# Modulation products of one decoder layer: the attention gate and the FFN shift and scale made on VectorE in 1024-column pieces, and four FFN block pairs split over two halves of their rows

## The chip, the cores and the metric

One core of a Trainium2 chip runs the whole layer as one program. The metric is the device time of one execution in microseconds; lower is better. Three executions of the kernel before took 1274.52, 1274.74 and 1276.62 us, median 1274.74 us.

## What is computed

One layer for 256 tokens of width 2048, all in float32. A conditioning vector `c` makes six modulation rows of 2048 numbers; they shift, scale and gate the attention part (`_a`) and the feed-forward part (`_f`).

```python
mod = jax.nn.silu(c) @ w_ada[l] + b_ada[l]          # w_ada: 2048 x 12288
shift_a, scale_a, gate_a, shift_f, scale_f, gate_f = jnp.split(mod, 6, axis=-1)
h = rms_norm(x, g_attn_pre) * (1 + scale_a) + shift_a
proj = h @ w_in                                      # 2048 x 5456
...                                                  # two kinds of attention, 8 heads each
x = x + gate_a * rms_norm(mixed @ w_o, g_attn_post)
h = rms_norm(x, g_ffn_pre) * (1 + scale_f) + shift_f
ff = (silu(h @ w_gate) * (h @ w_up)) @ w_down        # 2048 x 5632, and back
x = x + gate_f * rms_norm(ff, g_ffn_post)
```

## The kernel before, in words

**Weights.** Every weight matrix is read once from HBM, a megabyte at a time (`wload`, L148), into one of five `raw` buffers. ScalarE copies a K pair to `whi` in a reduced format (L168), VectorE makes the rest `wlo` by a subtraction (L169), and each product becomes three TensorE passes (`mm3`, L176 to L182). Three pairs of `whi`/`wlo` buffers exist, so VectorE can be at most three such tiles ahead of TensorE. One 512-column, four-K-tile load is 24 passes of 512 columns.

**Modulation.** `ada_block` (L191) queues the product of silu(c) with a block of `w_ada` columns as units of one megabyte, each a load and a use. With `on_pe` the use is done on TensorE: the K tiles go to four column groups of the array (L225), the four partial rows end in one PSUM bank, ScalarE brings them out (L242), and for a gate the bias row comes by one more product (L240). Without `on_pe` VectorE does it: one multiply-and-add per K tile over all 128 partitions into `aacc` (L231, L233). Either way a finishing product on TensorE sums over partitions: `ada_cols` (L275) makes columns of shift and gain*(1+scale) (L282 after TensorE, L286 after VectorE), `ada_gate` (L296) makes the gate row (L301). The attention's own shift and scale are always made on TensorE. Of the attention gate (`Ga`) blocks 0 and 1 are made on TensorE and 2 and 3 on VectorE; of the FFN shift and scale (`modF`) blocks 0, 1 and 3 on TensorE and 2 on VectorE; the FFN gate (`Gf`) wholly on VectorE. Blocks are 512 columns: a unit has four K tiles, and on VectorE four instructions.

**Order.** `ada_step` takes units off that queue: during the last `w_in` group one or two per weight block (`RATE`, L737), one per block in the output projection (`side`, L789), `FRATE` per block in the split FFN blocks (L884). While the last `w_in` group and the first two column blocks of `w_o` run, attention proceeds by stages (`attn_step`, L430): rotary embedding (`rope`, L351), indexer scores and top-k, softmax, products with V. Each engine runs its instructions in the order in which they stand; a scheduler with a timeline of its own sets that order when the program is built.

**From attention to FFN.** `tail_pair` (L770) ends `w_o` with token tile 0 first. `residual` (L836) then makes x1: the block times its gate (L768), the square sums, `ry`, x1 (L843), the diagonal matrix `dg` (L848). `h2_tiles` (L826) needs `dg`, and the FFN's first products need its result. `NSPLIT` gate/up column blocks are first multiplied with K tiles 0 to 7 alone (L875), put aside in `part` by ScalarE (L887), and completed later by a VectorE addition (L909); so the second half of `modF` may come late.

Of the kernel before, what the change touches and what calls it, by code (L numbers as in the profile page):

```python
# [22 lines left out]
P = 128  # L23
S = 256
T = 2
# [14 lines left out]
GA_DVE = (2, 3)  # L40
F_DVE = (2,)
# [3 lines left out]
FRATE = 2  # L45
# [4 lines left out]
NSPLIT = 2  # L50
# [6 lines left out]
def layer(ctx, tc, x, c, positions, w_ada, b_ada, g_attn_pre, g_attn_post, g_ffn_pre,  # L57
# [26 lines left out]
    # ---- constants  # L84
# [20 lines left out]
    # ---- vectors, brought to columns  # L105
# [33 lines left out]
    c33 = ct([P, KT, 33], "c33")  # L139
    POOL.memset(c33, 0.0)  # L140
    DVE.tensor_copy(c33[:, :, 1], csil)
# [5 lines left out]
    # ---- weights: fp32 tiles split exactly into two fp32r parts  # L147
    def wload(rows, k0, nk, c0, n, more=None):  # L148
        """Rows k0.. of a block of columns: {(K tile, 512-column block): (hi, lo)}."""
# [4 lines left out]
        for a in range(0, nk, 2):  # L154
            m = min(2, nk - a)
            step = min(n, 1024 // m)
            for b in range(0, n, step):
                w = min(step, n - b)
                if more is not None and a + m == nk:
                    hi = more.tile([P, 1024], F32R, tag="xhi", name=nm("xhi"))  # L160
                    lo = more.tile([P, 1024], F32R, tag="xlo", name=nm("xlo"))
# [22 lines left out]
    # ---- adaLN modulation  # L184
# [6 lines left out]
    def ada_block(col0s, n, on_pe, finish, brow=None):  # L191
        """Queues the products of silu(c) with n columns of w_ada at each of col0s, a megabyte at a
        time. On the tensor engine the K tiles go to four column groups, and the products of the
        i-th block end as the rows 32*j+i of one bank."""
# [5 lines left out]
        def new_acc(b):  # L200
            st["acc", b] = wp.tile([P, 512], F32, tag="aacc", name=nm("aacc"), bufs=2)

        def load(b, u):
            if u == 0 and brow is not None and (b == 0 or not on_pe):
                new_acc(b)
                if not on_pe:
                    POOL.memset(st["acc", b], 0.0)
                SP.dma_start(st["acc", b][0:1], brow)
# [65 lines left out]
    # shift and scale as columns: shift, and gain*(1+scale)  # L274
# [20 lines left out]
    # gate times the post gain, the same row on every partition  # L295
    def ada_gate(G, chunk, col, on_pe):  # L296
        c0 = chunk * D + col

        def finish(accs):
            ps = tr_bank()  # L300
            PE.matmul(ps, lhsT=ones, rhs=accs[0], start=True, stop=True)  # L301
            DVE.tensor_tensor(G[:, col:col + 512], ps, G[:, col:col + 512], op=ALU.mult)

        ada_block([c0], 512, on_pe, finish, b_ada[0:1, c0:c0 + 512])

    # ---- first norm, transposed
# [15 lines left out]
    def make_h(H, src, mod, k, qs=slice(0, S), lk=None, on_act=True):  # L322
        """A K tile of gain*(1+scale)*x + shift, split in two; the work shared by ACT and DVE."""
# [13 lines left out]
    ph1 = ExitStack()  # L337
# [646 lines left out]
```

## Time and profile before

| | |
|---|---|
| runs | 1274.52, 1274.74, 1276.62 us |
| profiled execution, first to last instruction (its span) | 1272.5 us |
| what lies around the span, taken from the median of the runs | 2.2 us |
| TensorE busy | 1233.9 us, 97% of the span |
| VectorE busy | 774.3 us, 61% |
| ScalarE busy | 560.9 us, 44% |
| DMA queue q1 | 309.14 MB, 70.7% of 16 engines |
| mean granted TensorE clock | 0.993 of full speed |

The execution that was profiled has no time of its own beside its span; the median of the runs is 2.2 us above that span. The busy time of TensorE is modelled at the ends of its matmuls, so a full row of nines says that it was always fed and not how fast it went; the starts of two neighbours in the order of time say that. An average such as VectorE's 61% covers stages with different limits, so the stages are read one by one below.

### The profile page before, as it was taken

To read this page: it belongs to the slowest core of one execution; us is meant where nothing else is said; L and a number is where in the kernel's file an instruction comes from. 1 tells how busy PE (TensorE), PEld (TensorE's weight loads), DVE (VectorE), ACT (ScalarE), POOL (GpSimd) and SP (SyncE) were. 2 spreads that over 40 slices of the span, in tenths; PEclk is the share of its full clock that TensorE was granted. 3 is DMA by queue.
4 is the path that set the end of the run, shared out by engine and by line. 5 is a ranking of instruction groups with operands and counts; after the bars stand their busy time and mean duration, and the time that the engine had idled before them with its cause. 6 is when DMAs were issued, how large, how long until landed. Compare 5 with 4: busy or idle time off the path is not lost.

```text
span 1272.5 us, 15272 instructions
## 1 busy us (share of the span) xinstructions
PE 1233.9 (97%) x5938; PEld 950.3 (75%) x5938; DVE 774.3 (61%) x1160; ACT 560.9 (44%) x806; POOL 21.4 (2%) x55
## 2 busy tenths in 40 slices
PE   4999999999999999899999999999999999999996
PEld 3666666777666786688887888888888888888885
DVE  3576455898598683758867545754455454445565
ACT  4733333345345543764444444444444334444442
POOL 1000000000000000200000000000000000000000
PEclk8999999999999999999999999999999999999998
DMA  9999997978687487858878656766556555565541
GB/s 307 339 343 327 347 381 278 314 263 321 211 285 268 142 329 289 306 167 286 282 264 290 200 193 222 251 227 198 176 189 199 190 188 190 194 198 182 184 164 66
DMA packets 160090, 310.13 MB, mean 244 GB/s; under 512 B 5785, under 2 KB 19978, under 8 KB 158738
## 3 DMA queue, kind: packets, MB, share of 16 engines
q1 hardware_dynamic: 159938, 309.14, 70.7%
q8 instruction: 46, 0.75, 0.2%
q14 instruction: 26, 0.21, 0.0%
q10 hardware_dynamic: 80, 0.02, 0.0%
HBM read 307.05 MB, written 2.10 MB: 243 GB/s over the span
## 4 chain that ended last, share of the span: by engine, by line
PE 88%; DMA 4%; DVE 4%; issue 1%; ACT 1%; SPq 1%; POOL 0%; DVEq 0%; POOLq 0%; ACTq 0%
PE mm L181 26%; PE mm L178 26%; PE mm L182 25%; PE ad L225 5%; DMA raw<-in_w_ada_dram 4%; DVE aacc L233 2%; DVE wlo L169 1%; PE tr L474 1%; PE tr L411 1%; PE tr L918 1%; PE tr L830 1%; SPq L211 1%; PE tr L392 1%; PE tr L301 0%; PE tr L282 0%
## 5 line engine op out<-in xcount | busy, mean ns | idle before, releaser
L169 DVE TENSOR_TENSOR wlo<-raw,whi 128x1024 fp32r<-128x1024 f32 (+1 forms) x383 | 462.3, 1212 | 338.6 <-ACT whi L168 337.7
L168 ACT ACTIVATE whi<-raw 128x1024 fp32r<-128x1024 f32 (+1 forms) x383 | 400.3, 1050 | 522.4 <-PE mm L182 458.1
L181 PE MATMUL mm<-wlo,h 128*128 128x512 f32 (+1 forms) x1056 | 416.8, 395 | 1.9 <-DVE wlo L169 1.9
L182 PE MATMUL mm<-whi,h 128*128 128x512 f32 (+1 forms) x1056 | 409.9, 389 | 0.2 <-DVE h L335 0.2
L178 PE MATMUL mm<-whi,h 128*128 128x512 f32 (+1 forms) x1056 | 381.4, 394 | 2.4 <-ACT h L330 1.4
L181 PEld LDWEIGHTS mm<-wlo,h 128*128 128x128 f32 x1056 | 198.9, 188 | 62.5 <-issue 9.5
L178 PEld LDWEIGHTS mm<-whi,h 128*128 128x128 f32 x1056 | 196.8, 188 | 63.2 <-issue 13.6
L182 PEld LDWEIGHTS mm<-whi,h 128*128 128x128 f32 x1056 | 198.3, 188 | 42.5 <-issue 3.0
L181 PE MATMUL mm<-wlo,gT 128*128 128x512 f32 x348 | 135.8, 390 | 0.0
L182 PE MATMUL mm<-whi,gT 128*128 128x512 f32 x348 | 135.4, 389 | 0.0
L178 PE MATMUL mm<-whi,gT 128*128 128x512 f32 x348 | 123.0, 390 | 0.0
L233 DVE SCALAR_TENSOR_TENSOR aacc<-raw,csil,aacc 128x512 f32<-128x512 f32 x126 | 94.1, 746 | 23.8 <-DMA raw<-in_w_ada_dram 22.5
L225 PE MATMUL ad<-raw,c 128*32 128x512 f32 (+2 forms) x640 | 79.6, 537 | 9.9 <-DMA raw<-in_w_ada_dram 9.9
L733 DVE TENSOR_TENSOR PR<-mm,PR 128x512 f32<-128x512 f32 (+1 forms) x88 | 57.1, 669 | 41.2 <-PE mm L182 41.0
L182 PEld LDWEIGHTS mm<-whi,gT 128*128 128x128 f32 x348 | 65.3, 188 | 13.8 <-issue 0.2
L181 PEld LDWEIGHTS mm<-wlo,gT 128*128 128x128 f32 x348 | 65.3, 188 | 13.7 <-issue 0.2
L178 PEld LDWEIGHTS mm<-whi,gT 128*128 128x128 f32 x348 | 65.3, 188 | 13.4
L181 PE MATMUL mm<-wlo,mixT 128*128 128x512 f32 x124 | 49.1, 397 | 0.0
L178 PE MATMUL mm<-whi,mixT 128*128 128x512 f32 x124 | 47.5, 400 | 0.6 <-ACT mixT L587 0.6
L182 PE MATMUL mm<-whi,mixT 128*128 128x512 f32 x124 | 46.4, 399 | 0.0
L225 PEld LDWEIGHTS ad<-raw,c 128*32 128x32 f32 x640 | 17.6, 116 | 36.4 <-issue 31.3
L181 PEld LDWEIGHTS mm<-wlo,mixT 128*128 128x128 f32 x124 | 23.3, 188 | 7.8 <-issue 2.5
(195 smaller groups left out, 678.8 us busy)
## 6 DMA issues: line engine op xcount, KB each, us to landing
raw<-in_w_ada_dram SPq DMA_DIRECT2D x96, 1024.0 KB, 7.1
raw<-in_w_gate_dram SPq DMA_DIRECT2D x44, 1024.0 KB, 5.2
raw<-in_w_up_dram SPq DMA_DIRECT2D x44, 1024.0 KB, 5.1
raw<-in_w_down_dram SPq DMA_DIRECT2D x44, 1024.0 KB, 5.2
raw<-in_w_in_dram SPq DMA_DIRECT2D x39, 1024.0 KB, 6.9
raw<-in_w_o_dram SPq DMA_DIRECT2D x16, 1024.0 KB, 5.0
xx<-in_x_dram SPq DMA_DIRECT2D x2, 1024.0 KB
x<-in_x_dram SPq DMA_DIRECT2D x2, 1024.0 KB, 4.7
```

The costliest lines, as they stand in the source:

```text
L168: ACT.activation(hv, src, AF.Copy)
L169: DVE.tensor_tensor(lv, src, hv.bitcast(F32), op=ALU.subtract)
L178: i = PE.matmul(ps, lhsT=hi, rhs=whi, start=start, stop=False)
L181: PE.matmul(ps, lhsT=hi, rhs=wlo, start=False, stop=False)
L182: PE.matmul(ps, lhsT=lo, rhs=whi, start=False, stop=stop)
L211: SP.dma_start(st[b, u], ada_w[u * kk * P:(u + 1) * kk * P, col0s[b]:col0s[b] + n] .rearrange("(k p) n -> p k n", p=P))
L225: PE.matmul(st["ps"][32 * j:32 * j + 32, :n], lhsT=c33[:, k, 1 - b:33 - b], rhs=w, start=(b == 0 and k < 4), stop=(b == nb - 1 and k >= 12 ...
L233: DVE.scalar_tensor_tensor(acc, w, csil[:, k:k + 1], acc, op0=ALU.mult, op1=ALU.add)
L392: PE.transpose(tr[:, i * P:(i + 1) * P], PR[:, t, c0:c0 + P], ident)
L411: PE.matmul(sc[i][:, SEG[t]], lhsT=st["q"][r, (2 * j + t) * P:(2 * j + t + 1) * P], rhs=ikT[r, :P * (t + 1)], start=True, stop=True)
L474: PE.matmul(sc[i][:, SEG[t]], lhsT=l, rhs=r, start=False, stop=(t == T - 1))
L733: DVE.tensor_tensor(dst, banks[c0][t][:, :n], dst, op=ALU.add)
```

## The change

Three things change, and some buffers are moved to make room.

1. `ada_gate` no longer takes a TensorE path, and `ada_cols` is called for the FFN with `on_pe` false. Blocks are 1024 columns, so a unit is two K tiles and two VectorE instructions. `aacc` holds 1024 columns. The FFN gate, on VectorE before too, is made in 1024-column pieces as well.
2. `NSPLIT` goes from 2 to 4, and `FRATE` from 2 to 1: all four gate/up column blocks of the first FFN group are split over two halves of their rows (K tiles 0 to 7, then 8 to 15).
3. Buffers: the two last tiles of a `tail_pair` share one tile with the second `part` buffer; the silu(c) columns `c33` take the place of `nsel` until top-k begins; the rotary temporaries take the two `on` buffers of the differential heads instead of one pair of their own.

```diff
-GA_DVE = (2, 3)
-F_DVE = (2,)
-FRATE = 2
+FRATE = 1
-NSPLIT = 2
+NSPLIT = 4
...
-                    hi = more.tile([P, 1024], F32R, tag="xhi", name=nm("xhi"))
-                    lo = more.tile([P, 1024], F32R, tag="xlo", name=nm("xlo"))
+                    both = more.tile([P, 2, 1024], F32R, tag="part", name=nm("xhl"))
+                    hi, lo = both[:, 0], both[:, 1]
...
-            st["acc", b] = wp.tile([P, 512], F32, tag="aacc", name=nm("aacc"), bufs=2)
+            st["acc", b] = wp.tile([P, 1024], F32, tag="aacc", name=nm("aacc"), bufs=2)
...
-    def ada_gate(G, chunk, col, on_pe):
+    def ada_gate(G, chunk, col, n):
         c0 = chunk * D + col
         def finish(accs):
-            ps = tr_bank()
-            PE.matmul(ps, lhsT=ones, rhs=accs[0], start=True, stop=True)
-            DVE.tensor_tensor(G[:, col:col + 512], ps, G[:, col:col + 512], op=ALU.mult)
-        ada_block([c0], 512, on_pe, finish, b_ada[0:1, c0:c0 + 512])
+            for a in range(0, n, 512):
+                ps = tr_bank()
+                PE.matmul(ps, lhsT=ones, rhs=accs[0][:, a:a + 512], start=True, stop=True)
+                g = G[:, col + a:col + a + 512]
+                DVE.tensor_tensor(g, ps, g, op=ALU.mult)
+        ada_block([c0], n, False, finish, b_ada[0:1, c0:c0 + n])
...
-        m1 = pp.tile([P, P], F32, tag="rp1", name=nm("rp1"), bufs=1)
-        m2 = pp.tile([P, P], F32, tag="rp2", name=nm("rp2"), bufs=1)
+        m = pp.tile([P, 2, P], F32, tag="on", name=nm("rp"), bufs=2)
+        m1, m2 = m[:, 0], m[:, 1]
...
-    for b in range(4):
-        ada_gate(Ga, 2, b * 512, b not in GA_DVE)
+    for b in range(2):
+        ada_gate(Ga, 2, b * 1024, 1024)
     need_ga = len(units)
-    for b in range(4):
-        ada_cols(modF, 3, bF, gF, b * 512, 512, b not in F_DVE)
-        if b == 1:
+    for b in range(2):
+        ada_cols(modF, 3, bF, gF, b * 1024, 1024, False)
+        if b == 0:
             need_f1 = len(units)
...
-            for b in range(4):
-                ada_gate(Gf, 5, b * 512, False)
+            for b in range(2):
+                ada_gate(Gf, 5, b * 1024, 1024)
```

The program that is built moves instructions. On VectorE, where attention's indexer scores (`score`) end and top-k is about to begin, this stood before (`wlo` are weight splits, `PR` the sums of the input projection):

```order
L447 COPY skT<-tr_2658 128x256
L422 SCALAR_TENSOR_TENSOR score<-rl_2654,iwS,score 128x128
L422 SCALAR_TENSOR_TENSOR score<-rl_2654,iwS,score 128x256
L448 TENSOR_TENSOR score<-score,mask 128x384
L422 SCALAR_TENSOR_TENSOR score<-rl_2711,iwS,score 128x128
L422 SCALAR_TENSOR_TENSOR score<-rl_2711,iwS,score 128x256
L169 TENSOR_TENSOR wlo_3141<-raw_3138,whi_3140 128x1024
L733 TENSOR_TENSOR PR<-mm_2940,PR 128x512
L169 TENSOR_TENSOR wlo_3145<-raw_3138,whi_3144 128x1024
```

And this stands there now, in the changed kernel's line numbers (`aacc` is a modulation product):

```order
L448 COPY skT<-tr_2600 128x256
L228 SCALAR_TENSOR_TENSOR aacc_2992<-raw_2990,csil,aacc_2992 128x1024
L422 SCALAR_TENSOR_TENSOR score<-rl_2592,iwS,score 128x128
L422 SCALAR_TENSOR_TENSOR score<-rl_2592,iwS,score 128x256
L228 SCALAR_TENSOR_TENSOR aacc_2992<-raw_2990,csil,aacc_2992 128x1024
L422 SCALAR_TENSOR_TENSOR score<-rl_2596,iwS,score 128x128
L422 SCALAR_TENSOR_TENSOR score<-rl_2596,iwS,score 128x256
L228 SCALAR_TENSOR_TENSOR aacc_2992<-raw_2995,csil,aacc_2992 128x1024
L485 TENSOR_REDUCE mx_2841<-tr_2832 128x1 x2
L449 TENSOR_TENSOR score<-score,mask 128x384
L164 TENSOR_TENSOR wlo_3268<-raw_3265,whi_3267 128x1024
```

The sixteen products of one whole modulation column block stand here, each between two steps of attention or two weight splits; before, no modulation product stood between the first score of this phase and the end of top-k.

On TensorE, where `w_o` ends and the FFN begins, this stood before (the last passes of `w_o`, modulation units, then the products with `dg`):

```order
L181 MATMUL mm_3923<-xlo_4194,mixT 128x512
L182 MATMUL mm_3923<-xhi_4193,mixT 128x512
L225 MATMUL ad_4170<-raw_4412,c_112 32x512 x4
L225 MATMUL ad_4170<-raw_4418,c_112 32x512 x4
L225 MATMUL ad_4170<-raw_4458,c_112 32x512 x4
L830 MATMUL tr_4283<-dg_3918,x_3897 128x128 x4
```

And now:

```order
L176 MATMUL mm_3824<-xhl_4070,mixT 128x512
L177 MATMUL mm_3824<-xhl_4070,mixT 128x512
L831 MATMUL tr_4159<-dg_3819,x_3798 128x128 x4
L831 MATMUL tr_4180<-dg_3819,x_3798 128x128 x4
L173 MATMUL mm_4249<-whi_4253,h_3814 128x512
```

The three modulation units are gone from between the last pass and the first product that waits for `dg`. On VectorE, in the `residual` of token tile 0 that makes this `dg` (`sst`, `rs` and `x` are its steps), this stood before:

```order
L768 TENSOR_TENSOR y<-mm_3922,Ga 128x512
L839 TENSOR_REDUCE sst<-ssy 128x1
L144 TENSOR_SCALAR rs_4228<-sst 128x1
L843 SCALAR_TENSOR_TENSOR x_3897<-y,ry,x_3897 128x1024 x2
L169 TENSOR_TENSOR wlo_4377<-raw_4374,whi_4376 128x1024
```

And now:

```order
L769 TENSOR_TENSOR y<-mm_3823,Ga 128x512
L840 TENSOR_REDUCE sst<-ssy 128x1
L228 SCALAR_TENSOR_TENSOR aacc_4049<-raw_4287,csil,aacc_4049 128x1024
L139 TENSOR_SCALAR rs_4104<-sst 128x1
L164 TENSOR_TENSOR wlo_4254<-raw_4251,whi_4253 128x1024
L228 SCALAR_TENSOR_TENSOR aacc_4049<-raw_4287,csil,aacc_4049 128x1024
L769 TENSOR_TENSOR y<-mm_3822,Ga 128x512
L844 SCALAR_TENSOR_TENSOR x_3798<-y,ry,x_3798 128x1024 x2
```

Two modulation products, a weight split and a block of token tile 1 now stand between the square sums and x1.

## Rows read from the trace of the kernel before

**Rows 1.** The page's head: busy time of the engines, and the span in 40 slices of 31.8 us, in tenths.
```profile
span 1272.5 us, 15272 instructions
PE 1233.9 (97%) x5938; PEld 950.3 (75%) x5938; DVE 774.3 (61%) x1160; ACT 560.9 (44%) x806; POOL 21.4 (2%) x55
PE   4999999999999999899999999999999999999996
DVE  3576455898598683758867545754455454445565
```

**Rows 2.** Busy time of each engine in four stretches: the last `w_in` group with attention and the first two columns of `w_o`; the rest of `w_o`, the residual and the first FFN products; the FFN's start; the rest of the span. Columns: stretch and length, busy us (instructions) of PE, PEld, DVE, ACT and POOL, granted clock, DMA share, GB/s.
```profile
198.00:450.00 252.00, 246.97 (x1278) 171.99 (x1270) 187.96 (x461) 113.28 (x248) 8.61 (x10) 1.00 0.74 258
450.00:533.00 83.00, 79.30 (x389) 57.41 (x388) 53.37 (x82) 40.17 (x71) 6.65 (x11) 1.00 0.86 317
533.00:577.00 44.00, 44.00 (x214) 36.95 (x214) 25.74 (x43) 28.38 (x48) 0.53 (x1) 1.00 0.58 193
577.00:1273.00 696.00, 684.77 (x3055) 565.51 (x3053) 397.24 (x401) 293.32 (x313) 2.17 (x4) 0.99 0.61 206
```

**Rows 3.** The modulation products on TensorE (L225) in two of these stretches: busy us (records) of PE and PEld. A unit of 512 columns is eight records.
```profile
198.00:450.00 252.00, 26.53 (x176) 4.21 (x168) 1.00 0.74 258
450.00:533.00 83.00, 11.23 (x64) 1.85 (x64) 1.00 0.86 317
```

**Rows 4.** One such unit among the passes of `w_in` on TensorE, in order of time: start us, us, what, count.
```profile
287.26 0.61 PE L178 MATMUL mm<-whi,h 128*128 128x512 f32 x2
287.80 1.06 PE L225 MATMUL ad<-raw,c 128*32 128x512 f32 x8
288.80 0.50 PE L181 MATMUL mm<-wlo,h 128*128 128x512 f32 x1
289.13 0.39 PE L182 MATMUL mm<-whi,h 128*128 128x512 f32 x1
```

**Rows 5.** Groups by line and shape: count, busy us, mean ns of one, idle before.
```profile
L240 PE MATMUL ad<-aacc,ident 1*32 1x512 f32 x4 | 2.1, 600 | 0.0
L286 PE MATMUL tr<-ones,aacc 128*128 128x1 f32 x16 | 2.1, 218 | 0.0
L843 DVE SCALAR_TENSOR_TENSOR x<-y,ry,x 128x1024 f32<-128x1024 f32 x4 | 5.0, 1281 | 1.8 <-POOL ry L145 1.8
L231 DVE TENSOR_SCALAR aacc<-raw,csil 128x512 f32<-128x512 f32 x2 | 1.0, 478 | 0.0
L313 DVE TENSOR_SCALAR xx<-xx,rx 128x2048 f32<-128x2048 f32 x2 | 2.5, 1283 | 0.8 <-POOL rx L145 0.8
L909 DVE TENSOR_TENSOR part<-mm,part 128x512 f32<-128x512 f32 x8 | 5.2, 681 | 0.0
```

**Rows 6.** The modulation products on VectorE (L233) as a whole, and their busy us (instructions) in four stretches.
```profile
L233 DVE SCALAR_TENSOR_TENSOR aacc<-raw,csil,aacc 128x512 f32<-128x512 f32 x126 | 94.1, 746 | 23.8 <-DMA raw<-in_w_ada_dram 22.5
198.00:450.00 252.00, 35.04 (x47) 1.00 0.74 258
450.00:533.00 83.00, 11.19 (x15) 1.00 0.86 317
577.00:1273.00 696.00, 47.83 (x64) 0.99 0.61 206
376.00:450.00 74.00, 11.21 (x15) 1.00 0.63 219
```

**Rows 7.** What VectorE waited for between 198 and 450 us (waited for: us in total, times, longest), the first rows.
```profile
DVE wlo L169 <- ACT whi L168: 36.7, 28, 4.5
DVE score L422 <- ACT rl L415: 6.0, 4, 3.3
DVE mx L484 <- PE tr L474: 4.6, 6, 2.0
```

**Rows 8.** Four short stretches and one longer, columns as in rows 2: VectorE's highest shares, its share in the middle of attention's end, and that end as a whole.
```profile
250.00:300.00 50.00, 50.00 (x254) 36.50 (x252) 46.41 (x117) 23.68 (x57) 3.54 (x4) 1.00 0.85 296
400.00:430.00 30.00, 25.00 (x137) 18.93 (x135) 23.10 (x60) 16.14 (x48) 2.11 (x2) 1.00 0.56 193
450.00:475.00 25.00, 25.00 (x118) 20.90 (x118) 23.55 (x31) 11.39 (x17) 0.00 (x0) 1.00 0.94 352
575.00:625.00 50.00, 50.00 (x228) 41.48 (x227) 46.36 (x57) 24.05 (x26) 0.00 (x0) 1.00 0.83 290
376.00:450.00 74.00, 68.97 (x385) 52.41 (x383) 53.28 (x137) 40.80 (x111) 3.86 (x4) 1.00 0.63 219
```

**Rows 9.** From the last pass of `w_o` to the first product with `dg`: TensorE, then VectorE's steps of the residual, in order of time; in brackets the idle time before and what ended it.
```profile
511.32 0.39 PE L182 MATMUL mm<-xhi,mixT 128*128 128x512 f32 x1
511.64 2.78 PE L225 MATMUL ad<-raw,c 128*32 128x512 f32 x24
516.57 0.38 PE L830 MATMUL tr<-dg,x 128*128 128x128 f32 x1 [2.15 <-POOL dg L848]
507.64 0.15 DVE L839 TENSOR_REDUCE sst<-ssy 128x1 f32<-128x4 f32 x1
507.82 0.15 DVE L144 TENSOR_SCALAR rs<-sst 128x1 f32<-128x1 f32 x1
508.64 2.48 DVE L843 SCALAR_TENSOR_TENSOR x<-y,ry,x 128x1024 f32<-128x1024 f32 x2 [0.66 <-POOL ry L145]
```

More of the change, by code (lines that the diff above doesn't have):

```diff
@@ L138, in layer @@
     ACT.activation(csil, cols[:, 0:16], AF.Silu)
-    c33 = ct([P, KT, 33], "c33")
-    POOL.memset(c33, 0.0)
-    DVE.tensor_copy(c33[:, :, 1], csil)
     def rstd(o, ss, n, width, eng=DVE):
@@ L206, in load @@
                 if not on_pe:
-                    POOL.memset(st["acc", b], 0.0)
-                SP.dma_start(st["acc", b][0:1], brow)
+                    POOL.memset(st["acc", b][:, :n], 0.0)
+                SP.dma_start(st["acc", b][0:1, :n], brow)
             raw = wp.tile([P, 2048], F32, tag="raw", name=nm("raw"), bufs=RAW)
@@ L293, in ada_cols @@
         ada_block([chunk * D + col, (chunk + 1) * D + col], n, on_pe, finish)
-    def ada_gate(G, chunk, col, on_pe):
+    def ada_gate(G, chunk, col, n):
         c0 = chunk * D + col
         def finish(accs):
-            ps = tr_bank()
-            PE.matmul(ps, lhsT=ones, rhs=accs[0], start=True, stop=True)
-            DVE.tensor_tensor(G[:, col:col + 512], ps, G[:, col:col + 512], op=ALU.mult)
-        ada_block([c0], 512, on_pe, finish, b_ada[0:1, c0:c0 + 512])
+            for a in range(0, n, 512):
[4 more added lines that the diff above has]
+        ada_block([c0], n, False, finish, b_ada[0:1, c0:c0 + n])
+    ph1 = ExitStack()
+    pp = ph1.enter_context(tc.tile_pool(name="pp", bufs=1))
+    c33 = pp.tile([P, 528], F32, tag="nsel", name="c33").rearrange("p (k n) -> p k n", n=33)
+    POOL.memset(c33, 0.0)
+    DVE.tensor_copy(c33[:, :, 1], csil)
     ssx = ct([P, T], "ssx")
@@ L335, in make_h @@
         DVE.tensor_tensor(lo, hf[:, :n], hi.bitcast(F32), op=ALU.subtract)
-    ph1 = ExitStack()
-    pp = ph1.enter_context(tc.tile_pool(name="pp", bufs=1))
     PR = pp.tile([P, T, NPROJ], F32, tag="PR", name="PR")
@@ L369, in layer @@
     score = pp.tile([P, 384], F32, tag="score", name="score")
-    nsel = pp.tile([P, 384], F32, tag="nsel", name="nsel")
     nselb = pp.tile([P, 384], BF16, tag="nselb", name="nselb")
@@ L441, in top_k @@
         m8 = pp.tile([P, T, 8], F32, tag="m8", name="m8")
+        nsel = pp.tile([P, 528], F32, tag="nsel", name="nsel")[:, :384]
         def head():
```

## The prediction

> **What bounds the kernel now.** I read the page's head first. TensorE is busy 1233.9 us of a span of 1272.5 us, and from the second to the last but one of the 40 slices it shows a nine or an eight; VectorE is at 61% [rows 1]. So over the span TensorE is the bound and a microsecond taken off it is worth a microsecond, as long as VectorE stays beneath it. But the change puts work on VectorE in one part of the span only, so I read busy time by stages [rows 2]. The reader is to see there that VectorE does 188.0 us in the 252 us from 198 to 450 us (75%) and 53.4 us in the 83 us that follow (64%), and that TensorE loses 5 us and 3.7 us in these two. After 577 us VectorE is at 57% under a TensorE that hardly stops. I call the two stretches A and B; everything that the change moves lies in them or costs nothing.
>
> **What leaves TensorE.** In A stand 176 records of modulation products, in B 64, eight to a unit: 22 units and 8 units [rows 3]. The change takes 32 units off (two blocks of the attention gate with four units, three FFN blocks with eight), so two lie ahead of 198 us. The price of one: from the start of a unit to the start of the next pass is 1.00 us, and from 287.26 to 289.13 us three passes and a unit took 1.87 us, where a pass among passes starts 0.23 us after the other; the unit with its borders costs 1.19 us [rows 4]. Between 1.0 and 1.2 I take 1.1: units that stand together have fewer borders. That is 24.2 us in A, 8.8 in B, 2.2 before. The two bias products go too, 2.1 us, in A [rows 5]. Added are twelve finishing products, since VectorE leaves a separate sum for shift and for scale (32 in place of 20): eight programmed products of this kind took 2.1 us, so 0.26 us each and 3.1 us in all, which I put in B [rows 5]. If nothing else mattered, the span would fall by 35.2 + 2.1 - 3.1 = 34.2 us.
>
> **What VectorE gets.** A product of 512 columns takes 746 ns [rows 6]; the multiply-and-add of the same kind over 1024 columns in the residual takes 1281 ns [rows 5], and I take that. The first K tile of a column block is a multiplication alone: 478 ns at 512 columns and 1283 ns at 2048, so between them at 1024; I take 0.75 us [rows 5]. By the order of the changed program, 58 modulation instructions (two of them multiplications) stand between the weight splits that start at 198 and 450 us before, and 32 (again two) between those that bound B.
> - A: 188.0 - 35.5 (the old products, multiplication included) + 56 x 1.281 + 2 x 0.75 = 225.7 us [rows 2, 6].
> - B: 53.4 - 11.7 + 30 x 1.281 + 2 x 0.75 = 81.6 us.
>
> TensorE by itself would need 252 - 24.2 - 2.1 = 225.7 us in A and 83 - 8.8 + 3.1 = 77.3 us in B. So VectorE draws level in A and passes TensorE in B, and no engine fills every gap of a stretch in which each waits for the other. **The bound moves to VectorE there**, and the time is its work divided by the share of the time that it can be busy, u.
>
> **What u is.** No stretch of this trace is set by VectorE alone for long, so I bound u. Its highest shares, with TensorE never short, are 92.8% (250 to 300 us), 94.2% (450 to 475) and 92.7% (575 to 625); its share where attention's steps wait for each other across engines, and TensorE with them, is 77% (400 to 430) [rows 8]. Most of its idle time in A is waiting for ScalarE's copy of a weight tile, 36.7 us, which is back pressure from TensorE and goes when VectorE is late; waits of attention, 6.0 and 4.6 us at the top, partly stay [rows 7]. I take 93%, the nearest of the full stretches, and let u run from 88% to 97.5%.
> - A at 93%: 242.7 us, 9.3 less than 252.
> - B at 93%: 87.7 us, 4.7 more than 83.
> - Before 198 us: 2.2 less.
>
> Sum: -6.8 us, span 1265.7 us, and with the 2.2 us that lie around it **1268 us**.
>
> **The rest of the change, at nothing.** From 577 us on, the FFN gate's 64 products become 32: 47.8 us become 41.0; eight more additions of `part` cost 5.4 us [rows 5, 6]; VectorE stays near 397 of 696 us under TensorE [rows 2]. If that cover went, it would be 5.4 us at most. The eight added copies to `part` are on ScalarE, at 42% there. The split itself gives TensorE no product more or fewer. The units' megabytes are the same, four bias rows in place of eight go through SP's queue, and POOL clears four tiles in place of six: nothing waits for either at present. `c33` is freed long before top-k needs its place. The second `part` buffer waits for `w_o`'s last pass, but is first written after two of the four split blocks. The rotary temporaries now wait for a differential head's transposes: below nothing excluded, since no path shortens; above, I bound it by the attention share of 77%, and it is in the slower case.
>
> **Rivals.**
> - *VectorE packs better, or TensorE stays the bound throughout.* At u = 97.5% A takes 231.5 and B 83.7 us: 1255 us; with no loss at all, 1272.5 - 34.2 + 2.2 = 1240.5 us. For it: the gaps of VectorE are mostly back pressure. Against it: 77% where attention ends.
> - *Attention's end becomes the bound (slower).* VectorE runs in order. In the changed order sixteen 1024-column products of one column block stand between indexer scores, top-k and the next weight splits, where none stood before, and TensorE has only a few `w_o` passes until these are through. The stretch from 376 to 450 us held 53.3 us of VectorE work with 15 old products, 11.2 us [rows 6, 8]; with sixteen new ones it is 62.1. At 93% it takes 66.7 us; at the 77% of its middle 80.6 us. That is 13.9 us more than in my sum: 1282 us. It decides from the point where this work gets under 81.7% (76.0 us), for then 9.3 us are lost and the time is 0.2% above the one before. The Trainium skill, page "Perfetto Trace Analysis", section "Optimizing Scalar/DVE Operations", speaks against the change here: larger operations help an engine that is saturated, but where VectorE is not saturated and holds others up, breaking instructions up may let work finish sooner. By that rule each of the sixteen holds what stands behind it by up to 1.281 - 0.746 = 0.535 us more, 8.6 us in all, and the sum would be 1276 us; no row here shows which of its two cases holds.
> - *Nothing measurable.* Where `w_o` ends, TensorE waits 2.15 us for `dg` after 2.8 us of modulation units [rows 9]; these units are gone, so it waits 4.9 us. On the way to `dg` two products, a weight split and a block now stand ahead of x1: 2 x 1.28 + 1.22 + 0.68 = 4.5 us, less the 0.66 us for which VectorE waited there anyway, 3.8 us more. TensorE would then wait 8.8 us. My B leaves room for 87.7 - 77.3 = 10.4 us of waiting, so this is within it; with another 7 us for token tile 1 and the first h2 tiles, which have products among them too, the gain is gone: 1275 us. The edge to no change lies where the 225.7 + 81.6 = 307.3 us of VectorE's work in A and B take 252 + 83 + 2.2 = 337.2 us, at u = 91.1%.
>
> **How the numbers follow.** About 0.2%, 2.5 us, is what a measurement of this kernel can tell from no change. u between 91.8% and 97.5% gives 1255 to 1272 us: 0.48. Better than that, down to 1240.5: 0.10. Within 2.5 us: 0.12. Slower, by attention's end or by u under 90.5%: 0.30. At 88% A takes 256.5 and B 92.7 us, 12 us above: 1287. The range from 1251 to 1287 us leaves out half of the best case and the worst of the slow one, some 0.17. Faster 0.58, same 0.12, slower 0.30.
>
> **What would show it.** In the profile of the changed kernel: no modulation unit on TensorE after some 190 us, new products at about 1.28 us, VectorE busy over 90% from about 190 to 510 us, and TensorE waiting there for `wlo` rather than VectorE for `whi`. A slice of eights or less on TensorE beside nines on VectorE is my case; nines on TensorE throughout would be the first rival. VectorE at 80% with TensorE short while top-k runs would be the slower one. After the first FFN products both kernels should take the same time to within 2 us. I would be wrong if a product took other than 1.2 to 1.35 us, or if VectorE waited in that stretch for DMA: in the trace of before 22.5 us of such waits stand, nearly all in the FFN [rows 6].

## The result and the profile after

Four executions took 1286.72 to 1289.33 us, median **1288.44 us**, beside 1275.52 us of the kernel before on the same chip: a ratio of 1.0109 (95% interval 1.0091 to 1.0127), 13 us slower. The time lies 1.4 us outside the range on record, on its slow side. The profiled execution spans 1285.8 us where before spanned 1272.5 us [rows 1].

The head of the page after, with the granted clock of TensorE in tenths as its last line:

```profile
span 1285.8 us, 14811 instructions
PE 1215.8 (95%) x5702; PEld 961.2 (75%) x5702; DVE 841.6 (65%) x1164; ACT 562.6 (44%) x809; POOL 25.9 (2%) x53
PE   4999999999986989699999999999999999999996
DVE  3576479999898577964588645675454454445565
PEclk9999999999977989899999999999999999999999
```

TensorE's busy time fell by 18.1 us and VectorE's rose by 67.3 us. In the 7th to 10th slices VectorE shows nines, and in the 12th to 17th slices, from some 354 to 546 us, TensorE has sixes and eights where it had nines, four of them with a clock below nine.

To see where the time went I cut both kernels at the same places: the starts of the 49th, 89th, 97th, 105th and 124th weight split on VectorE. The four stretches between are S1 (the last `w_in` group), S2 (the last indexer scores and top-k, in the changed kernel), S3 (the rest of attention under the first columns of `w_o`) and S4 (the rest of `w_o`, the residual, the first FFN block). The cuts follow the weights and not attention: before, top-k runs from 356.7 to 378.5 us, across the end of S1. So S1 and S2 are best read together. Columns as in [rows 2]. Before:

```profile
198.50:364.90 166.40, 166.40 (x832) 113.16 (x832) 125.77 (x295) 68.60 (x129) 4.76 (x6) 1.00 0.77 270
364.90:408.80 43.90, 42.63 (x233) 28.31 (x226) 35.65 (x103) 21.28 (x58) 2.80 (x3) 1.00 0.87 304
408.80:449.90 41.10, 37.34 (x212) 30.42 (x211) 26.44 (x67) 22.93 (x61) 1.05 (x1) 1.00 0.47 159
449.90:532.60 82.70, 79.00 (x387) 57.15 (x387) 53.07 (x82) 39.77 (x71) 6.65 (x11) 1.00 0.86 317
```

And after:

```profile
200.30:342.20 141.90, 136.86 (x641) 106.02 (x640) 135.80 (x250) 60.51 (x111) 4.91 (x4) 0.99 0.86 310
342.20:414.20 72.00, 55.91 (x231) 37.94 (x231) 62.77 (x162) 26.56 (x73) 3.08 (x3) 0.79 0.51 175
414.20:457.60 43.40, 40.97 (x249) 34.27 (x247) 23.52 (x60) 23.48 (x62) 0.69 (x1) 1.00 0.33 105
457.60:544.00 86.40, 71.95 (x300) 58.56 (x300) 76.80 (x91) 38.62 (x67) 8.87 (x10) 0.88 0.91 337
```

S1 gains 24.5 us, and VectorE is busy 96% of it. S2 loses 28.1 us: VectorE's work there went from 35.7 to 62.8 us, TensorE is short and its granted clock is 0.79. Together they are 3.6 us longer, for 37 us more of VectorE's work. S3 and S4 lose 2.3 and 3.7 us, what lies ahead of S1 1.8 us, and what lies behind S4 1.9 us. Here are the new products (L228) in the same four stretches, busy us and instructions:

```profile
200.30:342.20 141.90, 52.33 (x41) 0.99 0.86 310
342.20:414.20 72.00, 19.11 (x15) 0.79 0.51 175
414.20:457.60 43.40, 0.00 (x0) 1.00 0.33 105
457.60:544.00 86.40, 37.02 (x29) 0.88 0.91 337
```

Fifteen of them, 19.1 us, stand in S2 and none in S3, where VectorE is busy 54%. What S2 looks like on VectorE, in order of time (`m` and `nsel` are top-k's rounds, `s` the softmax weights of a differential head):

```profile
386.25 1.22 DVE L164 TENSOR_TENSOR wlo<-raw,whi 128x1024 fp32r<-128x1024 f32 x1
387.39 1.28 DVE L228 SCALAR_TENSOR_TENSOR aacc<-raw,csil,aacc 128x1024 f32<-128x1024 f32 x1
388.59 0.61 DVE L455 MAX8 m<-nsel 128x8 f32<-128x128 f32 x2
...
389.26 1.25 DVE L228 SCALAR_TENSOR_TENSOR aacc<-raw,csil,aacc 128x1024 f32<-128x1024 f32 x1
...
391.86 1.28 DVE L228 SCALAR_TENSOR_TENSOR aacc<-raw,csil,aacc 128x1024 f32<-128x1024 f32 x1
393.05 0.61 DVE L455 MAX8 m<-nsel 128x8 f32<-128x128 f32 x2
393.58 0.73 DVE L562 SCALAR_TENSOR_TENSOR s<-s,w 128x128 f32<-128x128 f32 x2
```

A product stands between the steps of the rounds shown, no row has idle time before it, and TensorE meanwhile waits for that `s`:

```profile
385.88 0.39 PE L572 MATMUL tr<-PR,pT 128*128 128x128 f32 x2
394.06 0.45 PE L496 MATMUL tr<-ident,s 128*128 128x128 f32 x1 [7.80 <-DVE s L562]
```

From the first step of top-k to its end VectorE is busy 98% of the time, TensorE 55%:

```profile
369.40:400.60 31.20, 17.14 (x70) 10.98 (x68) 30.44 (x86) 10.29 (x27) 1.66 (x1) 0.72 0.75 261
```

The last `w_in` pass ends at 349 us (376 before), but top-k ends at 400.6 us (378.5 before), and attention's last output, which `w_o` needs, at 459.4 us (452.6 before).

At the end of `w_o` the forecast wait for `dg` is there, on TensorE first, then on VectorE, where two products, a weight split and a block of token tile 1 stand ahead of x1:

```profile
518.47 0.39 PE L177 MATMUL mm<-xhl,mixT 128*128 128x512 f32 x1
526.17 3.78 PE L831 MATMUL tr<-dg,x 128*128 128x128 f32 x16 [7.31 <-POOL dg L849]
514.85 1.28 DVE L228 SCALAR_TENSOR_TENSOR aacc<-raw,csil,aacc 128x1024 f32<-128x1024 f32 x1
517.24 1.28 DVE L228 SCALAR_TENSOR_TENSOR aacc<-raw,csil,aacc 128x1024 f32<-128x1024 f32 x1
519.03 2.47 DVE L844 SCALAR_TENSOR_TENSOR x<-y,ry,x 128x1024 f32<-128x1024 f32 x2
```

It is 7.31 us where 2.15 us stood before [rows 9].

### The profile page after: what moved, and what is told of

The parts are those of the page before. It is cut to its first block, busy times and chain, and to the rows that moved or that the text cites. A ratio compares the mean times of both kernels' runs of the same rounds, so it can differ in the third digit from the quotient of the medians.

```text
span 1285.8 us, 14811 instructions
## 1 busy us (share of the span) xinstructions
PE 1215.8 (95%) x5702; PEld 961.2 (75%) x5702; DVE 841.6 (65%) x1164; ACT 562.6 (44%) x809; POOL 25.9 (2%) x53
## 4 chain that ended last, share of the span: by engine, by line
PE 65%; DVE 4%; issue 2%; ACT 1%; DMA 1%; POOL 1%; DVEq 0%; POOLq 0%; ACTq 0%
PE mm L176 20%; PE mm L173 20%; PE mm L177 20%; DVE aacc L228 1%; DMA raw<-in_w_o_dram 1%; PE tr L831 1%; PE tr L919 1%; DVE wlo L164 1%; PE tr L475 1%; PE tr L411 0%; PE tr L297 0%; DVE nsel L456 0%; ACT whi L163 0%; PE tr L392 0%; DVE mx L485 0%
## 5 line engine op out<-in xcount | busy, mean ns | idle before, releaser
L176 PEld LDWEIGHTS mm<-wlo,h 128*128 128x128 f32 x1056 | 199.5, 189 | 63.5 <-DVE wlo L164 12.3
L228 DVE SCALAR_TENSOR_TENSOR aacc<-raw,csil,aacc 128x1024 f32<-128x1024 f32 x124 | 158.6, 1279 | 12.4 <-DMA raw<-in_w_ada_dram 11.5
L177 PEld LDWEIGHTS mm<-whi,gT 128*128 128x128 f32 x348 | 65.3, 188 | 14.1 <-issue 0.5
L176 PEld LDWEIGHTS mm<-wlo,gT 128*128 128x128 f32 x348 | 65.3, 188 | 13.9 <-issue 0.5
L173 PEld LDWEIGHTS mm<-whi,gT 128*128 128x128 f32 x348 | 65.3, 188 | 13.5
L176 PE MATMUL mm<-wlo,mixT 128*128 128x512 f32 x124 | 52.3, 423 | 2.5 <-DVE wlo L164 2.5
L173 PE MATMUL mm<-whi,mixT 128*128 128x512 f32 x124 | 49.1, 421 | 4.0 <-ACT whi L163 3.4
L177 PE MATMUL mm<-whi,mixT 128*128 128x512 f32 x124 | 48.9, 420 | 0.0
L220 PE MATMUL ad<-raw,c 128*32 128x512 f32 (+2 forms) x384 | 38.0, 474 | 10.8 <-DMA raw<-in_w_ada_dram 10.8
L173 PEld LDWEIGHTS mm<-whi,mixT 128*128 128x128 f32 x124 | 24.8, 203 | 11.0 <-ACT whi L163 4.2
```

What stands on the lines that cost most here:

```text
L173: i = PE.matmul(ps, lhsT=hi, rhs=whi, start=start, stop=False)
L176: PE.matmul(ps, lhsT=hi, rhs=wlo, start=False, stop=False)
L177: PE.matmul(ps, lhsT=lo, rhs=whi, start=False, stop=stop)
L220: PE.matmul(st["ps"][32 * j:32 * j + 32, :n], lhsT=c33[:, k, 1 - b:33 - b], rhs=w, start=(b == 0 and k < 4), stop=(b == nb - 1 and k >= 12 ...
L228: DVE.scalar_tensor_tensor(acc, w, csil[:, k:k + 1], acc, op0=ALU.mult, op1=ALU.add)
```

## The experiments

Medians in us; the ratio is to the kernel before on the same chip (median 1273.9 to 1275.5), with its 95% interval. The lengths of S1 to S4 are worked out from the starts of the same five weight splits in each profile; the last column is VectorE's busy time in S1 and S2 together.

| kernel | median | ratio | S1 | S2 | S3 | S4 | VectorE S1+S2 |
|---|---|---|---|---|---|---|---|
| before | 1274.5 | | 166.3 | 44.0 | 41.1 | 82.7 | 161.4 |
| changed | 1288.4 | 1.0109 (1.0091 to 1.0127) | 141.9 | 72.0 | 43.5 | 86.4 | 198.6 |
| e1 split alone | 1280.9 | 1.0055 (1.004 to 1.007) | 169.3 | 46.3 | 41.3 | 83.2 | 160.5 |
| h1 rotary buffers alone | 1279.2 | 1.0035 (1.0023 to 1.0046) | 169.3 | 46.3 | 41.4 | 83.1 | 160.5 |
| h3 split, own rotary buffers | 1277.3 | 1.0017 (1.0008 to 1.0027) | 166.5 | 43.9 | 41.3 | 84.0 | 161.4 |
| h2 changed, own rotary buffers | 1291.3 | 1.0139 (1.0119 to 1.016) | 143.2 | 74.1 | 43.4 | 88.7 | 198.6 |
| e5 changed, split undone | 1291.7 | 1.0132 (1.0115 to 1.015) | 142.0 | 73.4 | 43.0 | 92.3 | 198.5 |
| g1 gate alone | 1278.7 | 1.0036 (1.0024 to 1.0047) | 167.6 | 44.2 | 42.4 | 83.1 | 173.7 |
| g2 FFN alone | 1290.5 | 1.0134 (1.0111 to 1.0157) | 177.3 | 37.6 | 45.9 | 90.2 | 190.7 |
| e4 512 columns | 1291.9 | 1.014 (1.0124 to 1.0157) | 177.9 | 40.2 | 44.2 | 88.1 | 204.8 |
| e7 15 products out in S2 | 1276.9 | 1.002 (1.0011 to 1.003) | 139.2 | 64.5 | 43.3 | 86.7 | 181.3 |
| e8 15 products out ahead | 1280.8 | 1.0053 (1.0038 to 1.0068) | 141.9 | 65.3 | 43.1 | 85.5 | 183.1 |
| e6 held back | 1290.0 | 1.0117 (1.0098 to 1.0136) | 126.8 | 76.9 | 43.0 | 100.1 | 181.3 |
| p4 attention faster | 1294.4 | 1.0147 (1.0125 to 1.0168) | 159.9 | 58.3 | 43.8 | 89.1 | 198.1 |
| n1 products out | 1250.7 | 0.9816 (0.9802 to 0.9831) | 144.6 | 43.0 | 39.8 | 79.9 | 135.1 |
| k1 units out of before | 1252.3 | 0.9824 (0.9804 to 0.9843) | 148.0 | 48.5 | 39.8 | 78.7 | 163.0 |
| k3 all on TensorE | 1300.8 | 1.0199 (1.0177 to 1.0222) | 190.4 | 45.0 | 43.5 | 83.1 | 136.7 |
| m1 units whole | 1263.9 | 0.9917 (0.99 to 0.9933) | 163.1 | 44.1 | 41.3 | 80.6 | 161.4 |
| m3 all on TensorE, whole | 1279.2 | 1.0039 (1.0025 to 1.0052) | 177.6 | 37.9 | 45.3 | 82.4 | 135.7 |
| m4 gate on VectorE, whole | 1264.3 | 0.9917 (0.99 to 0.9933) | 163.8 | 42.8 | 41.4 | 79.0 | 173.1 |

**One part of the change at a time.** My first theory: VectorE's products ahead of the end of top-k cost what was lost. The rivals: the split or the shared buffers; any product; the length of a piece.

```diff
# e1: before, with NSPLIT = 4, FRATE = 1 and the changed buffers of the tail and the rotary temporaries (c33 as before)
# g1: before
-GA_DVE = (2, 3)
+GA_DVE = (0, 1, 2, 3)
# g2: before
-F_DVE = (2,)
+F_DVE = (0, 1, 2, 3)
# e4: the changed kernel, its blocks of 1024 columns made 512 (Ga, modF, Gf)
```

> The modulation as before (same blocks on TensorE and VectorE, 512 columns), with NSPLIT 4, FRATE 1 and the moved buffers. Theory (VectorE's products ahead of the end of top-k cost what the change lost): 1273 to 1278 us, no change, since no product moves between the engines. Rival (the split, its extra copies and additions, or the shared buffers cost it): 1283 to 1289 us.

> Only the attention gate's first two blocks go from TensorE to VectorE, in 512-column pieces; the rest as before. VectorE gets 32 x 0.746 = 23.9 us in the stretch ahead of top-k, TensorE loses 8 units and two bias products, 10.9 us. Theory (VectorE has room ahead of top-k, so work put there is hidden): 1264 to 1271 us. Rival (a product on VectorE always costs more than the TensorE work that it replaces): 1280 to 1288 us.

> Only the FFN shift's and scale's blocks 0, 1 and 3 go to VectorE, in 512-column pieces; gate and split as before. 96 products of 0.746 us come, 24 units leave TensorE. Theory (products that stand between indexer scores and the end of top-k cost their time): 24 of them stand there, 18 us, and the time is 1284 to 1296 us. Rival (long pieces are what holds attention up): with short pieces 1268 to 1278 us.

> The changed kernel with all of VectorE's modulation in 512-column pieces: two products of 0.746 us for each of 1.281 us, some 20 us more of VectorE work ahead of the FFN. Theory (VectorE's amount of work sets the time): 1298 to 1310 us. Rival (the length of a piece, 0.535 us more for each of sixteen, is what costs): 1278 to 1284 us.

e1 took 1280.9 us, between the two: something beside the products costs 6 to 7 us. `c33` stays in its own place in e1, so its sharing was never run by itself. g1 took 1278.7 us, against the theory and short of the rival: the gate's 32 products were not hidden. g2's 1290.5 us lie where the theory had them, but not for its reason: S1 and S2 together are only 4.6 us longer than before, S3 and S4 12.3 us. e4 took 1291.9 us, between the two: some 19 us more of VectorE work up to the end of S4 cost 3.5 us.

**The buffers, and products left out at two places.**

```diff
# h1: before; h2 is the changed kernel with the opposite edit
-        m1 = pp.tile([P, P], F32, tag="rp1", name=nm("rp1"), bufs=1)
-        m2 = pp.tile([P, P], F32, tag="rp2", name=nm("rp2"), bufs=1)
+        m = pp.tile([P, 2, P], F32, tag="on", name=nm("rp"), bufs=2)
+        m1, m2 = m[:, 0], m[:, 1]
# e7 (b == 1) and e8 (b == 0): the changed kernel without these products
-                else:
+                elif not (brow is None and b == 1 and col0s[0] == 3 * D):
                     DVE.scalar_tensor_tensor(acc, w,
# h3: e1 with m1, m2 of their own
```

> The kernel before with one edit: the rotary temporaries take the two buffers of the differential heads' output. Theory now (this sharing reorders attention under the last w_in group, and that is what the split kernel lost between 280 and 440 us): 1279 to 1282 us. Rival (that loss belongs to the split or the other buffers): 1273 to 1276 us.

> The changed kernel with the rotary temporaries in two buffers of their own again (the angles' temporaries lie in an attention buffer to make room). If the sharing's cost is added to that of the products: 1281 to 1284 us. If VectorE's products hide it, since in this kernel attention waits for VectorE anyway: 1286 to 1290 us.

> The changed kernel without 15 products of 1.281 us: those of the FFN scale's first block (its first K tile alone is left), which stand between indexer scores and the end of top-k. Theory (each product there costs its whole time): 15 x 1.281 = 19.2 us less, 1267 to 1272 us. Rival (attention's own chain or TensorE's lower clock sets that stretch): 1281 to 1288 us.

> The changed kernel without 15 other products: those of the FFN shift's first block, which stand in the 55 us ahead of that stretch, beside w_in. Theory (TensorE was busy 136.9 of the 141.9 us ahead of top-k, so little can be had there, and what is had waits at top-k): 1281 to 1288 us. Rival (VectorE is the bound in the whole stretch, so any 15 products are worth the same): 1267 to 1272 us.

> The split over four block pairs, FRATE 1 and the moved c33 and tail tiles, with the modulation as before and the rotary temporaries in buffers of their own; TensorE's order is that of the kernel before up to the end of w_o. The split alone is the difference of 7.0 us (split with shared temporaries) and 4.5 us (shared temporaries alone), 1275 to 1279 us; if the split is free, 1273 to 1275.5 us.

h1 took 1279.2 us: the shared rotary buffers cost 4.5 to 5 us by themselves, in S1 and S2, and h3 leaves 2 to 3 us to the split, all of it behind S3. In the changed kernel own buffers gave nothing back (h2, 2.9 us slower, with intervals that overlap): what they cost has no place there, for a reason that m1 below shows. e7 gave 11.6 us for 19.2 us of products, between theory and rival. e8 gave 7.6 us, 0.2 us more than its theory allowed, 6.7 of it in S2: S1 is as long as with the products. In e7 top-k ends at 381.4 us, 19.2 us earlier, to the tenth what was left out; but attention's last output comes only 10.4 us earlier.

**Is TensorE or attention the bound before?** I now thought that attention's chain sets S1 to S3 in both kernels.

```diff
# k1: before, of the gate's and the FFN's units on TensorE only K tiles 0 to 3 of each (of shift and scale: of the shift)
+                    if col0s[0] >= 2 * D and (b > 0 or k > 3):
+                        continue
# k3: before
-GA_DVE = (2, 3)
-F_DVE = (2,)
+GA_DVE = ()
+F_DVE = ()
# e6: the changed kernel
-RATE = (1, 1, 1, 2)
+RATE = (1, 1, 1, 0)
+SIDE = (0, 0, 0, 2, 2, 2, 2, 2, 2, 2, 2, 2, 2, 2)   # units at each w_o block, in place of 1
```

> The kernel before, without most of the modulation products that TensorE makes for the attention gate and the FFN (27 of the 32 units that the change moves; only K tiles 0 to 3 of each are left); nothing is added to VectorE. Theory now (attention's own chain ends the stretch under the last w_in group in the kernel before too, so that TensorE's units there filled time that it would have waited): some 2 us ahead of 198 us, 2 to 6 in attention, 8 behind it: 1258 to 1264 us, and attention's last output at most 6 us earlier. Rival (TensorE is the bound there, as the prediction had it): 27 x 1.1 = 29.7 us less, 1243 to 1248 us.

> The change turned round: the kernel before with all of the attention gate and of the FFN shift and scale on TensorE, 14 to 16 units more (15.4 to 17.6 us); VectorE loses 62 products, 46 us, half of them ahead of top-k. If TensorE bounds the stretch: 1287 to 1293 us. If attention's chain through VectorE bounds it, the added units fill waiting and the chain gets shorter: 1270 to 1282 us.

> The changed kernel with the modulation's units held back: 17 in place of 27 under the last w_in group, none at the first three blocks of w_o, two at each later one. By the order six products fewer stand at top-k and eight fewer ahead of it, and twelve more right behind it, where VectorE was at 62%. Theory (what stands ahead of attention's end costs about 0.5 of its time, 14 x 1.281 x 0.5 = 9 us, and the twelve are hidden): 1276 to 1282 us. Rival (only the sum of VectorE's work counts): 1286 to 1291 us.

That theory fell: k1 took 1252.3 us, 22 us less, 0.82 us for each of the 27 units, and attention's last output came 15.9 us earlier, where the theory allowed 6. k3 took 26.4 us more. So TensorE is the bound before, if not for every unit's whole time: k1 lies between theory and rival. But sixteen units cost 1.65 us each in k3, which nothing explained yet. e6, with 1290.0 us, fell where its rival had it. Yet half of its theory holds: it gained 10.2 us in S1 and S2, and S3 took 13.5 us more VectorE work in the same 43 us. Then S4 lost 13.7 us, with no more VectorE work than before the edit. Two units at a block come as runs of products, VectorE in S4 of e6:

```profile
479.20 5.25 DVE L229 SCALAR_TENSOR_TENSOR aacc<-raw,csil,aacc 128x1024 f32<-128x1024 f32 x4
485.87 1.23 DVE L165 TENSOR_TENSOR wlo<-raw,whi 128x1024 fp32r<-128x1024 f32 x1 [1.42 <-ACT whi L164]
```

While a run lasts no weight tile is split, and behind it VectorE itself waits for one. This is a part of the loss at most: TensorE's idle time in S4 is 19.0 us in place of 14.5, and for the rest it has more to do there, since attention's last output now comes 6.3 us behind the start of S4 (1.8 in the changed kernel). How much the runs cost was not tested. e5 points the same way: with two units at a split block S4 is 92.3 us.

**The price of a unit on either engine.** The trace of before showed units parted by other work. TensorE in S1 of before:

```profile
204.42 1.06 PE L225 MATMUL ad<-raw,c 128*32 128x512 f32 x6
205.41 0.50 PE L181 MATMUL mm<-wlo,h 128*128 128x512 f32 x1
...
207.91 1.05 PE L225 MATMUL ad<-raw,c 128*32 128x512 f32 x2
208.88 1.04 PE L240 MATMUL ad<-aacc,ident 1*32 1x512 f32 x2
...
224.33 1.07 PE L225 MATMUL ad<-raw,c 128*32 128x512 f32 x8
225.33 0.33 PE L392 MATMUL tr<-ident,PR 128*128 128x128 f32 x1
```

Two records hold TensorE for 0.97 us, six for 0.99 us, all eight of a unit for 1.00 us. From the start of S1 on, before had 13 parted runs, h1 19, k3 36.

```diff
# m1: before; m3 and m4 are k3 and g1 with it
+                    with (tc.high_priority() if i else nullcontext()):   # products 2 to 4 of a unit
                         PE.matmul(st["ps"][32 * j:32 * j + 32, :n], ...
# n1: the changed kernel
-                else:
+                elif not 2 * D <= col0s[0] < 5 * D:
                     DVE.scalar_tensor_tensor(acc, w,
```

> The kernel before with one edit: the four products of a modulation unit on TensorE follow each other without other work between them (in the kernel before the order parts a good part of them, and each part takes 0.98 us as the whole does). From 180 us on 33 units took 41.3 us in 34 runs; whole they would take some 32. If TensorE's time there is on the path: 1264 to 1269 us. If the parted units filled waiting: 1272 to 1276 us.

> The same with whole units, and the attention gate and FFN shift and scale wholly on TensorE: 16 units more, some 15 us, and 64 products, 47 us, fewer on VectorE. If a microsecond of VectorE's work costs 0.45 us in this stretch, as the runs so far have it: 6 us less than with whole units alone, 1258 to 1264 us. If VectorE's work is hidden while TensorE is full: 15 us more than that, 1278 to 1284 us.

> The changed kernel without its modulation products on VectorE for the attention gate and the FFN (only the first K tile of each shift and scale block is left): 92 products of 1.281 us, 118 us. If these products are the cost: 1246 to 1256 us, what the kernel before took without its units, less 5 units, plus what split and shared temporaries cost alone. If much of the loss lies in the order of attention or in the split: 1262 to 1272 us.

Products 2 to 4 of a unit are given precedence in m1, so that nothing comes between them. m1 took 1263.9 us: with whole units the kernel before is 10.0 us faster, and faster than either kernel of this case. From the start of S1 on, 29 units hold TensorE for 37.3 us before and for 30.4 us in m1; in k3 45 units hold it for 64.1 us, 26.8 us more than before, near k3's loss of 26.4. (Another 3.1 us of m1's gain lie ahead of S1.) The unit that stands there as six and two records, in m1:

```profile
201.30 1.06 PE L226 MATMUL ad<-raw,c 128*32 128x512 f32 x8
202.30 0.50 PE L181 MATMUL mm<-wlo,h 128*128 128x512 f32 x1
```

m3 costs 15.2 us more than m1, 0.95 us for each of sixteen units; the 47 us that VectorE no longer has to do are worth nothing there. And h1's loss is explained in part: it has 19 parted runs in place of 13, and its 29 units hold TensorE 2.9 us longer. That share the changed kernel, without such units, cannot have; the other 2 us stay open. n1 took 1250.7 us. So the change without its products is 23.2 us faster than the kernel before, and the products take 37.7 us back, for their 118 us: that is the loss. Its four stretches:

```profile
198.60:343.20 144.60, 140.83 (x679) 107.26 (x678) 100.53 (x234) 65.89 (x122) 2.77 (x4) 1.00 0.90 333
343.20:386.30 43.10, 40.24 (x196) 29.80 (x195) 34.57 (x120) 21.65 (x62) 2.07 (x3) 0.96 0.62 224
386.30:426.10 39.80, 37.37 (x216) 30.61 (x214) 23.76 (x61) 23.43 (x61) 0.69 (x1) 1.00 0.54 182
426.10:506.00 79.90, 72.49 (x339) 60.92 (x340) 44.13 (x66) 39.29 (x69) 5.22 (x10) 0.94 0.88 318
```

S1 takes no less time without its 52 us of products: TensorE is busy 97% of it, and attention's steps move up into it (some 16 us of VectorE's work). S2 takes 28.9 us less, S1 and S2 together 26.2 us, S3 3.6 us, S4 6.5 us.

**Three more runs.** m4 is g1 with whole units; e5 is the changed kernel with `NSPLIT = 2` and `FRATE = 2`; p4 is the changed kernel with `ATT = 2` in place of 1.

> Whole units, and the attention gate's first two blocks on VectorE in 512-column pieces. 24 more products stand ahead of the first indexer scores, none more at top-k; 8 units of 0.95 us and two bias products leave TensorE, 9.7 us. If products ahead of top-k are free as long as attention's steps keep their place (they do here, by the order): 1254 to 1260 us. If VectorE's 17.9 us more ahead of the first scores put attention off: 1264 to 1272 us.

> The changed kernel with two of attention's stages in place of one between weight blocks: the same work, but the first indexer scores stand 6 weight splits earlier in VectorE's order, and top-k two; top-k still ends behind 60 products. If the place of attention's steps in VectorE's order is what costs: 1276 to 1284 us. If the amount of work alone counts: 1287 to 1290 us.

> The changed kernel with two block pairs split over their rows in place of four, and two units at a block in place of one. If the split costs 2.9 us here as it did alone: 1284 to 1287 us. If its cost is hidden or given back by the modulation being spread thinner: 1287 to 1291 us.

m4 is no faster than m1: TensorE lost 8 units and S1 and S2 fell by 0.6 us, with VectorE at 84% of them. So 32 more products on VectorE, 24 us, took back the 9.7 us that TensorE was to be spared. Putting attention's steps earlier in VectorE's order did not help either: in p4 the scores come earlier, but top-k ends later; S1 and S2 together take 218.2 us with the same VectorE work, and it is slower. e5 is 3.3 us slower than the changed kernel, with intervals that overlap. It undoes the split and doubles the units at a block at once, so which of the two costs is not shown.

## Why the prediction was wrong

- **The products' price held.** 1.281 and 0.75 us were taken, and the VectorE work of A and B came out at 222.1 and 76.8 us (forecast 225.7 and 81.6):

```profile
L228 DVE SCALAR_TENSOR_TENSOR aacc<-raw,csil,aacc 128x1024 f32<-128x1024 f32 x124 | 158.6, 1279 | 12.4 <-DMA raw<-in_w_ada_dram 11.5
L226 DVE TENSOR_SCALAR aacc<-raw,csil 128x1024 f32<-128x1024 f32 x4 | 3.0, 745 | 0.0
```

- **The bound moved to VectorE in part only.** In S1 and S2 it is busy 198.6 of 213.9 us, 93%, the u of the forecast. But this is partly luck: S1 stands at 96% and S2 at 87%, and in S1 TensorE is busy 96% too. Were the time VectorE's work divided by 0.93, a microsecond of work less would give 1.08 us. e7 and e8 took 17.3 and 15.5 us of it out of S1 and S2, which gave 10.2 and 6.7 us: 0.59 and 0.43 us each.
- **The step that failed is "A at 93%: 242.7 us".** I divided all of A's work by one u, as if products could stand anywhere in A. S3, 41.1 us of A before, got none, and VectorE's share there is 54% after (64% before). By S1 and S2 at 93% and S3 as it was, (222.1 - 23.5) / 0.93 + 41.1 = 254.6 us; measured were 257.3. So 11.9 of A's miss of 14.6 us are this one step, and 2.3 us the longer S3. Where products stand could have been read ahead of time from the same order that gave their number. e6 bears it out: with 13.5 us of VectorE's work put into S3, which got no longer, A takes 246.7 us, 10.6 less than in the changed kernel. (Its S4 then lost 13.7.) S3 of e6:

```profile
403.80:446.80 43.00, 37.23 (x207) 29.62 (x205) 37.08 (x74) 23.25 (x61) 1.80 (x2) 1.00 0.69 233
```

- **B held, by two errors that cancel**: 87.7 us forecast, 86.4 measured, but at 89% in place of 93%, and of 4.8 us less work. The wait for `dg` is 7.3 us where I had worked out 8.8.
- **Ahead of 198 us** I counted 2.2 us gained and 1.8 us were lost. n1 gains nothing there either (198.6 us).
- **The rest "at nothing"** took 1.9 us more. By h3 the split alone costs 2 to 3 us. My bound, 5.4 us, held; the cover was not whole.
- **TensorE's floor** was 34.2 us by 1.1 us a unit; n1 gives 23.2 us less than before (1273.9 us beside it). A unit that leaves is not worth the time that it held: 0.82 us in k1. In n1 TensorE stands idle 16.5 us of the four stretches, 8.7 before, and the split costs its 2 to 3 us.
- **The signs.** VectorE was to be busy over 90% from 190 to 510 us; it was 87%. TensorE was to wait there for `wlo` rather than VectorE for `whi`, and it came the other way round. In that stretch the two waited in all, us, times and longest:

```profile
DVE wlo L164 <- ACT whi L163: 19.2, 15, 6.5
PE mm L176 <- DVE wlo L164: 6.7, 4, 3.0
```

- **The rivals.** "Attention's end becomes the bound" comes nearest: VectorE holds TensorE up while top-k runs, and top-k ends 22.1 us later than before. But the rival's price rested on a VectorE at 77% of that time, and it was at 98%; what was long was its work, with products between attention's steps. I priced it at 1282 us; it had a chance of 0.30 and belonged ahead of the forecast. The other rival's 1255 us leaves out my own 2.2 us ahead of 198 us; by the forecast's terms it is 1252.7 us. The rule cited with the slower rival, from the Trainium skill, "Perfetto Trace Analysis", section "Optimizing Scalar/DVE Operations", would have shorter instructions end the bubbles where VectorE is not saturated. In e4 top-k does end 7.1 us earlier than in the changed kernel, but attention's last output comes 4.5 us later, and the kernel is 3.5 us slower. Its S2 of 40.2 us beside an S1 of 177.9 says little by itself, since most of top-k stands ahead of the cut there; together they are 4.2 us longer, for 6.2 us more of VectorE's work, as two pieces of 746 ns are dearer than one of 1279. VectorE is busy 94% of the two: this is the rule's saturated case, and the trace agrees with it there.

What the exchange comes to: a whole unit costs TensorE 0.95 us. On VectorE it is two products, 2.56 us, and in S1 and S2 of the changed kernel a microsecond of VectorE's work costs 0.43 to 0.59 us (e8, e7), so 1.1 to 1.5 us. m4 against m1 comes to some 0.4 us, at a VectorE share of only 84%. The units that the kernel before already has on VectorE are cheap, because TensorE covers them (m3 against m1); the next 32 are not.

What stays open: why e7 gives back 8.8 of the 19.2 us behind top-k, why a microsecond of VectorE's work costs about half of itself, what the lower granted clock (0.79 in S2, 0.88 in S4) costs by itself, and whether holding units back without runs (e6 with one unit at a block) would gain. None of these was tried.

## What to carry to other kernels

Before dividing a stretch's work by a share, look where in the changed order the added instructions stand, and cut the stretch there: room in a part where nothing stands is no room. Price a move between engines at the margin, on both: what leaves a full engine is worth its time only until the other fills, and here the last microseconds on that one cost about half of themselves. Look for operations that a scheduler has parted: keeping four products together gained 10 us, more than the 6.8 us that the change was forecast to gain.

## What the runs showed of the hardware

**A run of products on TensorE's column groups takes the same time whatever part of a unit it holds.** 0.97 us for two records, 1.00 us for eight, so each parting costs about a whole unit's time again (keeping units whole gave 10.0 us, m1). The Trainium skill, page "TensorE: Matmul & The Clock Gate", section "Why this matters for your kernels", says that products whose outputs lie in distinct groups of 32 partitions run side by side. The trace agrees.

**The granted clock fell where TensorE was not idle.** The sixteen finishing products of one shift and scale block, 32 records of a single column, stand behind attention in the changed kernel. TensorE in order of time, and the granted clock (third column from the right) in two stretches of 4 us:

```profile
454.94 2.74 PE L281 MATMUL tr<-ones,aacc 128*128 128x1 f32 x24
...
458.83 0.63 PE L176 MATMUL mm<-wlo,mixT 128*128 128x512 f32 x1
459.26 0.63 PE L177 MATMUL mm<-whi,mixT 128*128 128x512 f32 x1
```

```profile
454.00:458.00 4.00, 4.00 (x35) 3.95 (x36) 1.52 (x2) 2.49 (x3) 0.00 (x0) 1.00 0.52 179
458.00:462.00 4.00, 4.00 (x13) 3.10 (x12) 4.00 (x7) 0.00 (x0) 0.00 (x0) 0.57 1.00 412
```

Right behind them the clock is mostly at its lower level, 1.2 GHz, and passes start 0.43 us after each other in place of 0.23, some eight of them: some 1.6 us, on top of 3.7 us for the sixteen products. The same 32 records stand ahead of the same fall in n1, e7 and e8 (0.57 to 0.66 over the 4 us behind them); that they cause it was not tested by an edit. Their own price, 0.23 us each, is near the 0.26 us of the forecast; the slower passes behind them were not in it.
